# A hybrid attention block: the RMS norm's weight row multiplied into x instead of into every weight

## The chip, the cores and the metric

The kernel runs on one core of one Trainium2 chip. The metric is the device time of one launch in microseconds (us). The engines are called by the profile's names: PE (TensorE; PEld is its weight load), DVE (VectorE), ACT (ScalarE), POOL (GpSimd) and SP (SyncE, which issues the DMAs here).

## The reference

One layer of an encoder block on x of 2048 tokens by 1024 columns, all float32:

```python
def rms_norm(x, gain):
    y = x * lax.rsqrt(jnp.mean(x * x, axis=-1, keepdims=True) + EPS)
    return y * gain

h = rms_norm(x, norm_gain)            # norm_gain: 1024 numbers, one per column
proj = h @ w_in                       # 1024 x 8448: q, k, v of two mixers, gates, merge logits
# A: 8 query heads, 2 key/value heads of 64, window +-128, a sink logit
# B: 3 groups of 8 heads, (window, dilation) = (128,1), (512,4), (2048,16), joined by softmax denominators
# q and k: RMS norm per head; relative position bias; y = attention * silu(gate path)
merged = sigmoid(mg0 + b0) * (ya @ w_branch_a) + sigmoid(mg1 + b1) * (yb @ w_branch_b)
out = x + merged @ w_out
```

Since `h @ w = (x / rms) @ (gain[:, None] * w)`, the norm's weight row can be multiplied into the rows of w or into the columns of x.

## The kernel before

**Precision.** Matrix products of float32 operands are made of three float16 products: each operand is split into a high part (scaled by a power of two and rounded) and a low part (what is left). XH and XL hold the two parts of the normalized, transposed x for the whole run (columns of x on the partitions, 8 chunks, tokens along the free dimension); `wh`/`wl` and `gh`/`gl` hold those of a piece of weights.

**Start: x is prepared.** x comes in 16 tiles of 128 tokens by 1024 columns (`x_load`, 512 KB each, 14 buffers). For each tile:

- `x_square` (L427, ACT) sums the squares of each token; `x_stats` (L431, L240, DVE) and `x_newton` make the reciprocal root for a group of tiles: tiles 0 and 1, tiles 2 and 3, then groups of four. For the groups of two the Newton steps run on DVE (L254 to L256), for the groups of four on POOL (L249 to L252).
- `x_scale` (L441, DVE) multiplies the tile in place by the tokens' factors.
- `x_turn` (L447, PE) transposes it in two halves into PSUM (3 buffers `s`); `x_hi` (L450, ACT) writes XH and `x_lo` (L454, DVE) XL.

Between the transposes PE already works: the first two chunks of gate weights (`g_load`, `graw`) are prepared, and their products with the finished quarters of x (`g_step`, L288) are interleaved with the transposes of the next tiles.

**Weights.** Weights come in units of 384 columns (`w_units`, 14 of them, one attention head group each, then `w_mrg` for the merge gates) and in gate chunks of 128 columns (`w_gate`). Each is loaded raw in float32 (`w_load`, `g_load`), multiplied in place by the norm's weights `gn` (`w_gain`, L159, four pieces of two chunks of rows; `g_gain`, L303, two pieces of four; both on POOL), squared and summed on ACT (`w_square`, L198; `g_square`, L311), summed over the partitions by a matmul with ones (`norm_sum`, L173, on PE), turned into a power-of-two scale on DVE (`norm_pow`), and split (`w_hi`, L215, ACT; `w_lo`, L221, DVE; `g_hi`, `g_lo`, L333). The scale's inverse goes into later factors (`wsc`, `ih`, `im`, `imh`), and the unit's scale into the epsilon of the head norm (`sig`).

**Units.** While PE projects unit u (L617), the steps of unit u+1's weights run on the other engines. For each pair of token blocks the projections leave PSUM (L635, L647, L653), the q and k norms run (squares L660, sums L665, Newton steps on POOL, product L677 on DVE, head gain L684 on POOL, split L690 and L694, copies L699), and the transposed pieces feed the scores (L767), maxima (L782), exponentials (L790), splits (L795, L799) and values (L816). The branch outputs are gated by `YPart` (L882).

**End.** After the units, the products with the branch and merge weights (L288 into `fps`) and the output projection (L1254) follow.

**Order.** From the start to the end of the units every engine's instructions stand in an order that the code writes: each step is put into one heap with a planned time (`at(time, step)`), and steps are emitted in order of these times. Each engine then works through its own list in order. `chain` keeps the steps of one piece of weights in sequence. The x steps are planned by X_SQ, X_ST and X_CH: the first statistics at 7.8, the first scale at 9.3, each next scale 2.65 later. The loads are planned at .01 times the tile number; the load of `gn` (4 KB, 32 bytes to each partition) stands between the second and the third x tile, the first gate chunk behind the fourth. The part after the units is ordered by the framework's scheduler from its own estimates.

Of the kernel before, what the change touches and what calls it, by code (L numbers as in the profile page):

```python
# [21 lines left out]
F32 = mybir.dt.float32  # L22
# [3 lines left out]
OP = mybir.AluOpType  # L26
# [13 lines left out]
VSC = 2.0 ** -20  # L40
SX = 2.0 ** 10
SE = S + 256
# [36 lines left out]
X_G = (7.5, 15.282, 45.87)  # L79
X_GP = (2.1, 5.694, 7.094, 7.694, 8.894, 10.194)  # L80
X_W = (14.0, 38.0, 48.0, 1.1, 4.8, 5.2, 6.3, 0.6, 50.255)
X_TH = (0.8, 2.173, 3.5)
# [9 lines left out]
def block_kernel(tc, x, w_units, w_gate, w_mrg, w_out, w_bra, gain, qkg, sink, bias_a, bias_b, b_merge, out):  # L92
# [32 lines left out]
    XL = xp.tile([128, NCH, SE], F16, name="XL")  # L125
    gn = cst.tile([128, NCH], F32, name="gn")

# [20 lines left out]
    def w_load(u, parts=(0, 1, 2, 3)):  # L148
# [4 lines left out]
        for i in parts:  # L153
            nc.sync.dma_start(out=raw[:, 2 * i:2 * i + 2, :], in_=src[:, 2 * i:2 * i + 2, :])

    def gains(raw, c0, n):

        v = raw[:, c0:c0 + 2, :n]
        G.tensor_tensor(v, v, gn[:, c0:c0 + 2].unsqueeze(2).to_broadcast([128, 2, n]), OP.mult)  # L159

    def w_gain(u, i):
        gains(wtiles[u][0], 2 * i, 384 if u < NU else 256)

# [61 lines left out]
    def w_scale(u):  # L225
        for i in range(4):
            w_gain(u, i)
            w_square(u, i)
        for f in (w_sum, w_pow):
            f(u)  # L230
# [69 lines left out]

    def g_gain(c, i):
        v = gw[c][0][:, 4 * i:4 * i + 4, :]
        G.tensor_tensor(v, v, gn[:, 4 * i:4 * i + 4].unsqueeze(2).to_broadcast([128, 4, 128]), OP.mult)  # L303

    def g_square(c):
# [14 lines left out]
    def g_pow(c):  # L320
        raw, gh, gl, ps = gw[c]
        s, inv = norm_pow(ps)
        ih = ucol()
        V.tensor_scalar(ih[:], inv[:], 0.5 / SX, None, OP.mult)
        gw[c] = (gh, gl, ih, raw, s)
# [113 lines left out]
    def x_scale(t):  # L439
        i = t - groups[t][0]  # L440
        V.tensor_scalar(xts[t][:], xts[t][:], xss[groups[t]][:, i:i + 1], None, OP.mult)  # L441

# [34 lines left out]
    for t in range(XT_BUFS):  # L477
        at(.01 * t, x_load, t)
    at(.015, lambda: nc.sync.dma_start(out=gn[:], in_=gain))
    at(.035, g_load, 0)  # L480
# [27 lines left out]
    for c in range(3):  # L508
        b = X_G[c]
        if c == 2:  # L510
            at(X_G[0] + X_GP[5] + .1, g_load, c)
        chain([(b + X_GP[0] * i, g_gain, c, i) for i in range(2)]
              + [(b + d, f, c) for d, f in zip(X_GP[1:], (g_square, g_sum, g_pow, g_hi, g_lo))])
    at(X_W[0], w_load, 0)
    steps = [(X_W[2] + X_W[4], w_sum, 0), (X_W[2] + X_W[5], w_pow, 0)]
    for i in range(4):
        steps += [(X_W[1] + 1.9 * i, w_gain, 0, i), (X_W[2] + X_W[3] * i, w_square, 0, i),
                  (X_W[2] + X_W[6] + X_W[3] * i, w_hi, 0, i), (X_W[2] + X_W[6] + X_W[7] + X_W[3] * i, w_lo, 0, i)]
# [32 lines left out]
    class Unit:  # L551
# [20 lines left out]
        def scales(self):  # L572
            s, inv = wtiles[self.u][1:3]
            sig = sm.tile([128, 1], F32, name="sig")
            V.tensor_scalar(sig[:], s[:], SX, None, OP.mult)
# [4 lines left out]
            V.tensor_scalar(self.wsc[:], inv[:], 2.0 ** 6 / SX, None, OP.mult)  # L580
            ws[UNITS[self.u]] = self.wsc
# [478 lines left out]
    while t < NPAIR or heap or any(k >= t for k in fill):  # L1060
# [38 lines left out]
        if t == NPAIR - 2:  # L1099
            V.tensor_scalar(imh[:], wtiles[NU][2][:], 0.5 / SX, None, OP.mult)  # L1100
        t += 1
# [80 lines left out]
    for dc in (1, 2, 3, 4, 5, 6, 7, 0):  # L1182
# [3 lines left out]
        if own:  # L1186
            im = ucol()
            V.tensor_scalar(im[:], wtiles[u][2][:], 0.5 / SX, None, OP.mult)
        for q in range(4):
# [103 lines left out]
def _layout(x, norm_gain, w_in, q_norm_a, k_norm_a, q_norm_b, k_norm_b, sink_a, rel_bias,  # L1293
# [18 lines left out]
    bm = b_merge[0].reshape(2, 8, 128).transpose(2, 0, 1).reshape(128, 16)  # L1312
    return [x[0], w_units, w_gate, w_mrg, wo, w_bra, norm_gain.reshape(NCH, 128).T, qkg, sink_a, bias_a, bias_b, bm]

# [19 lines left out]
```

## Time and profile before

| | |
|---|---|
| time, three runs | 2017.61, 2019.15, 2013.93 us |
| median | 2017.61 us |
| span of the profiled execution (no other time is listed for it) | 2015.2 us |
| busy: PE, DVE, ACT, POOL | 1965.1, 1265.5, 1004.8, 839.3 us |
| instructions | 47585 |
| mean granted TensorE clock | 0.993 |

In rows of instructions, the first number is the start in us after the span's start, the second the duration in us; then engine, line, operation, tiles (out<-in), shapes and count; in brackets the engine's idle time before the instruction and what ended it. In lists of waits, the numbers are the total in us, how often, and the longest. In rows of stretches, the length comes first, then the busy time of PE, PEld, DVE, ACT and POOL with the count of instructions, then the granted clock, the DMA engines' share and GB/s.

### The profile page before, as it was taken

The page shows a single profiled execution, that of the slowest core. Times are in us where ns is not written, and L with a number is a line of the kernel's source. Part 1 is how long each engine was busy: PE and PEld are TensorE (multiplying, and loading weights), DVE is VectorE, ACT ScalarE, POOL GpSimd, SP SyncE. Part 2 cuts the span into 40 slices and gives each one's busy share as a digit, 9 for nine tenths or more (in the row PEclk, how much of TensorE's full clock was granted, in tenths as well). Part 3 has the DMA queues.
Part 4 walks back from the last instruction along what each step waited for, and adds up shares of the span by engine and source line. Part 5 has one row for each costly group of instructions (what it writes and reads, how often), then busy time and mean ns, then how long its engine had stood idle before and what let it go on. Part 6 is the DMA issues. An engine that isn't in the chain of part 4 may idle for free.

```text
span 2015.2 us, 47585 instructions
## 1 busy us (share of the span) xinstructions
PE 1965.1 (98%) x17666; PEld 1399.8 (69%) x17666; DVE 1265.5 (63%) x3456; ACT 1004.8 (50%) x2357; POOL 839.3 (42%) x2351
## 2 busy tenths in 40 slices
PE   6999999999999999999999999999999999999999
PEld 4567886678878898788989889896434444444444
DVE  6678877887768876677767877668572322254211
ACT  6467656765655566555666556565362221121100
POOL 4254556455647665566666666666200000000000
PEclk8999999999999999999999999999999999999999
DMA  6249976896659687486966857567551110046832
GB/s 243 79 92 175 171 151 142 152 191 142 167 117 174 134 162 155 97 178 119 183 118 133 183 119 160 99 140 169 149 182 42 48 49 31 27 141 205 268 122 89
DMA packets 560249, 276.97 MB, mean 137 GB/s; under 512 B 457744, under 2 KB 512144, under 8 KB 558480
## 3 DMA queue, kind: packets, MB, share of 16 engines
q1 hardware_dynamic: 560016, 273.93, 59.8%
q8 instruction: 138, 2.26, 0.5%
q14 instruction: 95, 0.78, 0.1%
HBM read 115.23 MB, written 48.50 MB: 81 GB/s over the span
## 4 chain that ended last, share of the span: by engine, by line
PE 79%; POOL 5%; DMA 5%; DVE 5%; issue 4%; ACT 2%; SPq 0%; POOLq 0%; DVEq 0%; ACTq 0%
PE pj L617 32%; PE fps L288 15%; PE pj L288 14%; PE fps L1254 8%; PE s L767 4%; PE pv L816 4%; DVE rw L677 1%; POOL rs_t L249 1%; POOL rs_t L250 1%; POOL rw L684 1%; DVE qss L665 1%; DMA fg<-ytd 1%; POOL rs_t L251 1%; PE s L447 1%; DMA graw<-in_w_gate_dram 1%
## 5 line engine op out<-in xcount | busy, mean ns | idle before, releaser
L617 PE MATMUL pj<-wl,XH 128*128 128x128 f16 (+2 forms) x2816 | 714.6, 268 | 0.0
L617 PE MATMUL pj<-wh,XH 128*128 128x128 f16 (+2 forms) x2816 | 708.4, 268 | 4.0 <-DVE vt L653 4.0
L617 PE MATMUL pj<-wh,XL 128*128 128x128 f16 (+2 forms) x2816 | 712.2, 269 | 0.0
L617 PEld LDWEIGHTS <-XH 128*128 128x128 f16 x5632 | 577.8, 113 | 66.8 <-issue 4.7
L617 PEld LDWEIGHTS <-XL 128*128 128x128 f16 x2816 | 316.8, 113 | 26.0
L782 DVE CUSTOM_DVE_ANT_0 pr<-s,b,ubuf 128x256 f32<-128x256 f32 (+3 forms) x512 | 218.7, 464 | 63.9 <-PE s L767 62.0
L288 PEld LDWEIGHTS <-wh 128*128 128x128 f16 x1280 | 125.7, 99 | 153.7 <-issue 7.7
L249 POOL TENSOR_TENSOR rs_t<-rs_y 128x8 f32<-128x8 f32 (+2 forms) x345 | 108.4, 314 | 209.1 <-DVE rs_y L240 151.8
L799 DVE SCALAR_TENSOR_TENSOR p<-pr,p 128x512 f16<-128x512 f32 (+2 forms) x256 | 184.2, 719 | 6.4 <-ACT p L795 5.3
L159 POOL TENSOR_TENSOR wraw<-wraw,gn 128x768 f32<-128x768 f32 (+1 forms) x80 | 108.3, 1360 | 170.5 <-DMA wraw<-in_w_mrg_dram 170.3
L684 POOL TENSOR_TENSOR rw<-rw,g 128x128 f32<-128x128 f32 (+1 forms) x224 | 137.8, 635 | 82.0 <-DVE rw L677 67.7
L1204 DVE SCALAR_TENSOR_TENSOR fg<-fg,fps 128x512 f32<-128x512 f32 x64 | 43.4, 685 | 202.7 <-PE fps L288 187.2
L677 DVE TENSOR_TENSOR rw<-rw,qr 128x512 f32<-128x512 f32 (+1 forms) x112 | 114.7, 1024 | 87.7 <-POOL vt L646 56.0
L795 ACT ACTIVATE p<-pr 128x512 f16<-128x512 f32 (+2 forms) x256 | 159.1, 622 | 11.0 <-DMA pt<-p 4.7
L635 ACT ACTIVATE rw<-pj 128x256 f32<-128x256 f32 (+1 forms) x224 | 86.6, 386 | 140.5 <-PE pj L617 136.5
L767 PE MATMUL s<-kq 128*128 128x128 f16 (+1 forms) x1856 | 147.3, 218 | 2.8 <-DMA kq<-spl 2.8
L767 PEld LDWEIGHTS <-kq 128*128 128x128 f16 x2016 | 130.1, 98 | 25.1 <-issue 3.0
L288 PE MATMUL pj<-XH,gh 128*128 128x512 f16 x384 | 146.9, 382 | 0.0
L288 PE MATMUL pj<-XL,gh 128*128 128x512 f16 x384 | 146.8, 382 | 0.0
L288 PE MATMUL pj<-XH,gl 128*128 128x512 f16 x384 | 146.6, 382 | 0.0
L699 POOL COPY spl<-spl 128x256 f16<-128x256 f16 (+1 forms) x224 | 92.6, 443 | 126.2 <-DVE spl L694 121.6
L816 PEld LDWEIGHTS <-pt 128*128 128x128 f16 x3024 | 122.0, 97 | 24.3 <-DMA pt<-p 2.4
(182 smaller groups left out, 3644.9 us busy)
## 6 DMA issues: line engine op xcount, KB each, us to landing
wraw<-in_w_units_dram SPq DMA_DIRECT2D x56, 384.0 KB, 4.8
wraw<-in_w_mrg_dram SPq DMA_DIRECT2D x24, 384.0 KB, 4.3
zd<-z SPq DMA_DIRECT2D x128, 66.0 KB, 1.9
zz<-zd SPq DMA_DIRECT2D x64, 132.0 KB, 3.1
xt<-in_x_dram SPq DMA_DIRECT2D x16, 512.0 KB, 9.7
gtd<-yo SPq DMA_DIRECT2D x32, 256.0 KB, 3.1
yo<-gtd SPq DMA_DIRECT2D x32, 256.0 KB, 3.8
ytd<-yo SPq DMA_DIRECT2D x32, 256.0 KB, 4.1
```

What stands on the lines that cost most here:

```text
L159: G.tensor_tensor(v, v, gn[:, c0:c0 + 2].unsqueeze(2).to_broadcast([128, 2, n]), OP.mult)
L249: G.tensor_tensor(tv, yv, yv, OP.mult)
L288: out.append(lambda w=w, xx=xx, ch=ch, i=i: T.matmul(ps[:], lhsT=w[:, ch, c0:c0 + 128], rhs=xx[:, ch, ts], start=(i == 0), stop=(i == n - 1)))
L617: out.append(lambda lhs=lhs, rhs=rhs, ch=ch, a=a, b=b, k=k: T.matmul(ps[:, a:b], lhsT=lhs[:, ch, :], rhs=rhs[:, ch, a:b], start=(k == 0), ...
L677: V.tensor_tensor(q, q, self.rr[:, :n].unsqueeze(2).to_broadcast([128, n, HD]), OP.mult)
L684: G.tensor_tensor(q[:, i, :un.nq, :], q[:, i, :un.nq, :], g, OP.mult)
L767: T.matmul(self.sv[j][:, o:o + k1 - k0], lhsT=q[:, h, :], rhs=kt[:, un.nq + kh + v * un.nk, k0:k1], start=(v == 0), stop=(v == 1))
L782: V.tensor_tensor_reduce(out=self.pv[:, j, self.p0:self.p0 + W], in0=self.sv[j], in1=un.bias[:, self.h0 + j, self.b0:self.b0 + W], scale=I ...
L795: A.activation(self.sp[:, :128 * n], self.pr, AF.Copy, scale=PSC)
L799: V.scalar_tensor_tensor(self.sp[:, 128 * n:], self.pr, PSC, self.sp[:, :128 * n], OP.mult, OP.subtract)
L816: T.matmul(self.po[:, j, :w], lhsT=p[:, n * j + s, :], rhs=un.v[key][:, vh, c0:c0 + w], start=(k == 0 and s == 0), stop=(k == 2 and s == n ...
L1254: T.matmul(ps[:], lhsT=m[:, ch, k, 128 * t:128 * t + 128], rhs=woh[h][w][:, ch, :], start=(i == 0), stop=(i == 23))
```

## The change

All multiplications of weights by `gn` are taken out (`gains`, `w_gain`, `g_gain` and their places in the order). Instead the norm's weight row is loaded once, the same 1024 numbers to each of the 128 partitions (`gain_load`, 512 KB written, planned between the third and the fourth x tile). `gain_scale`, planned at 6.5, finds its largest magnitude, makes a power of two from it (`pow2`, five small instructions), scales the row, and keeps that power and its inverse in `gp2` and `gi2`. `x_scale` multiplies x by the token's factor and by this row in one instruction. Where a later factor held the old scale, the power of two comes in as a second scalar of the same instruction. SX is halved.

```diff
-SX = 2.0 ** 10
+SX = 2.0 ** 9
+X_GS = 6.5
...
-    def gains(raw, c0, n):
-        v = raw[:, c0:c0 + 2, :n]
-        G.tensor_tensor(v, v, gn[:, c0:c0 + 2].unsqueeze(2).to_broadcast([128, 2, n]), OP.mult)
-    def w_gain(u, i):
-        gains(wtiles[u][0], 2 * i, 384 if u < NU else 256)
...
     def w_scale(u):
         for i in range(4):
-            w_gain(u, i)
             w_square(u, i)
...
-    def g_gain(c, i):
-        v = gw[c][0][:, 4 * i:4 * i + 4, :]
-        G.tensor_tensor(v, v, gn[:, 4 * i:4 * i + 4].unsqueeze(2).to_broadcast([128, 4, 128]), OP.mult)
...
-        V.tensor_scalar(ih[:], inv[:], 0.5 / SX, None, OP.mult)
+        V.tensor_scalar(ih[:], inv[:], 0.5 / SX, gp2[0][:], OP.mult, OP.mult)
...
     def x_scale(t):
         i = t - groups[t][0]
-        V.tensor_scalar(xts[t][:], xts[t][:], xss[groups[t]][:, i:i + 1], None, OP.mult)
+        V.scalar_tensor_tensor(xts[t][:], xts[t][:], xss[groups[t]][:, i:i + 1], gb[:], OP.mult, OP.mult)
+
+    gb = sp0.tile([128, D], F32, name="gb")
+
+    def gain_load():
+        nc.sync.dma_start(out=gb[:], in_=gain.broadcast_to([128, D]))
+
+    def gain_scale():
+        m = sm.tile([128, 1], F32, name="gm")
+        V.tensor_reduce(m[:], gb[:], AX.X, OP.max, apply_absolute_value=True)
+        s, i = pow2(m[:], "x")
+        V.tensor_scalar(gb[:], gb[:], s[:], 2.0 ** -14, OP.mult, OP.mult)
+        gp2.append(ucol())
+        gi2.append(ucol())
+        V.tensor_scalar(gp2[0][:], i[:], 2.0 ** 14, None, OP.mult)
+        V.tensor_scalar(gi2[0][:], s[:], 2.0 ** -14, None, OP.mult)
...
-    at(.015, lambda: nc.sync.dma_start(out=gn[:], in_=gain))
+    at(.025, gain_load)
+    at(X_GS, gain_scale)
...
-            steps += [(t + W_STEP[2] - W_STEP[6] + W_STEP[3] * i, w_gain, u + 1, i),
-                      (t + W_STEP[2] + W_STEP[3] * i, w_square, u + 1, i),
+            steps += [(t + W_STEP[2] + W_STEP[3] * i, w_square, u + 1, i),
...
-              + [(t + G_PREP[1] + .1 * i, g_gain, c, i) for i in range(2)]
               + [(t + d, f, c) for d, f in zip(G_PREP[2:], (g_square, g_sum, g_pow, g_hi, g_lo))])
```

The start's own gains of unit 0 and of the first three gate chunks go in the same way; `sig`, `wsc`, `imh` and `im` get `gi2` or `gp2` as `ih` does.

More of the change, by code (lines that the diff above doesn't have):

```diff
@@ L125, in block_kernel @@
     XL = xp.tile([128, NCH, SE], F16, name="XL")
-    gn = cst.tile([128, NCH], F32, name="gn")
+    gp2, gi2 = [], []
     def pow2(mx, name):
@@ L511, in block_kernel @@
             at(X_G[0] + X_GP[5] + .1, g_load, c)
-        chain([(b + X_GP[0] * i, g_gain, c, i) for i in range(2)]
-              + [(b + d, f, c) for d, f in zip(X_GP[1:], (g_square, g_sum, g_pow, g_hi, g_lo))])
+        chain([(b + d, f, c) for d, f in zip(X_GP[1:], (g_square, g_sum, g_pow, g_hi, g_lo))])
     at(X_W[0], w_load, 0)
@@ L516, in block_kernel @@
     for i in range(4):
-        steps += [(X_W[1] + 1.9 * i, w_gain, 0, i), (X_W[2] + X_W[3] * i, w_square, 0, i),
+        steps += [(X_W[2] + X_W[3] * i, w_square, 0, i),
                   (X_W[2] + X_W[6] + X_W[3] * i, w_hi, 0, i), (X_W[2] + X_W[6] + X_W[7] + X_W[3] * i, w_lo, 0, i)]
@@ L574, in scales @@
             sig = sm.tile([128, 1], F32, name="sig")
-            V.tensor_scalar(sig[:], s[:], SX, None, OP.mult)
+            V.tensor_scalar(sig[:], s[:], SX, gi2[0][:], OP.mult, OP.mult)
             self.eps = ucol()
@@ L579, in scales @@
             self.wsc = ucol()
-            V.tensor_scalar(self.wsc[:], inv[:], 2.0 ** 6 / SX, None, OP.mult)
+            V.tensor_scalar(self.wsc[:], inv[:], 2.0 ** 6 / SX, gp2[0][:], OP.mult, OP.mult)
             ws[UNITS[self.u]] = self.wsc
@@ L1099, in block_kernel @@
         if t == NPAIR - 2:
-            V.tensor_scalar(imh[:], wtiles[NU][2][:], 0.5 / SX, None, OP.mult)
+            V.tensor_scalar(imh[:], wtiles[NU][2][:], 0.5 / SX, gp2[0][:], OP.mult, OP.mult)
         t += 1
@@ L1187, in block_kernel @@
             im = ucol()
-            V.tensor_scalar(im[:], wtiles[u][2][:], 0.5 / SX, None, OP.mult)
+            V.tensor_scalar(im[:], wtiles[u][2][:], 0.5 / SX, gp2[0][:], OP.mult, OP.mult)
         for q in range(4):
@@ L1312, in _layout @@
     bm = b_merge[0].reshape(2, 8, 128).transpose(2, 0, 1).reshape(128, 16)
-    return [x[0], w_units, w_gate, w_mrg, wo, w_bra, norm_gain.reshape(NCH, 128).T, qkg, sink_a, bias_a, bias_b, bm]
+    return [x[0], w_units, w_gate, w_mrg, wo, w_bra, norm_gain, qkg, sink_a, bias_a, bias_b, bm]
 _INS = ["x", "w_units", "w_gate", "w_mrg", "w_out", "w_bra", "gain", "qkg", "sink", "bias_a", "bias_b", "b_merge"]
```

## The prediction

> **What bounds the kernel now.** I read the profile page first, then the busy time of four stretches, then what TensorE (PE) waited for, and last the first 30 us instruction by instruction.
>
> ```profile
> span 2015.2 us, 47585 instructions
> PE 1965.1 (98%) x17666; PEld 1399.8 (69%) x17666; DVE 1265.5 (63%) x3456; ACT 1004.8 (50%) x2357; POOL 839.3 (42%) x2351
> ```
>
> PE is busy 98% of the span, so a faster POOL or a slower DVE counts only where PE stands still. The next rows give, for each stretch, its length and then the busy time of PE, PE's weight loads, DVE, ACT and POOL; the cuts are at PE's last long wait of the start (27.1), at the end of the gate matmuls that run while x is prepared (82.2), and near the end of the units (1460).
>
> ```profile
> 0.00:27.10 27.10, 7.59 (x35) 5.90 (x35) 15.72 (x44) 19.07 (x33) 11.37 (x26) 0.90 0.94 359
> 27.10:82.20 55.10, 55.10 (x295) 31.94 (x296) 42.77 (x96) 35.21 (x61) 17.12 (x34) 0.95 0.18 70
> 82.20:1460.00 1377.80, 1357.99 (x14833) 1115.81 (x14831) 1028.84 (x2984) 830.36 (x2040) 793.97 (x2276) 1.00 0.72 147
> 1460.00:2015.20 555.20, 544.47 (x2508) 246.20 (x2506) 178.15 (x333) 120.14 (x224) 16.80 (x16) 0.99 0.34 110
> ```
>
> PE is idle for 19.5 us before 27.1, never in the next 55 us, for 19.8 us in the 1378 us of the units (1377.80 less 1357.99) and for 10.7 us after. The first idle time has one cause, in the list of PE's waits:
>
> ```profile
> PE s L447 <- DVE xt L441: 18.3, 4, 10.1
> ```
>
> In four waits, one of 10.1 us, PE stands before the transposes (L447) of an x tile that DVE has not yet scaled (L441). From 27.1 on PE never catches up, since it has no idle time to give back: **what the change adds to the way to the fifth scaled tile lengthens the whole kernel one for one.**
>
> **What is removed.** The multiplications by `gn` are all on POOL (min/median/max in ns, then first and last start in us):
>
> ```profile
> L159 POOL TENSOR_TENSOR wraw<-wraw,gn x80: 1037/1467/1917, 47.8 to 1636.4; 128x768 f32<-128x768 f32 x56, 128x512 f32<-128x512 f32 x24
> L303 POOL TENSOR_TENSOR wraw<-wraw,gn x18: 1030/1042/1488, 170.2 to 1376.0; 128x512 f32<-128x512 f32 x18
> L303 POOL TENSOR_TENSOR graw<-graw,gn x6: 1037/1041/1486, 10.9 to 55.4; 128x512 f32<-128x512 f32 x6
> L479 SPq DMA_DIRECT2D gn<-in_gain_dram x1: 424/424/424, 1.7 to 1.7; - x1
> ```
>
> That is 104 instructions. At about 1.4 us for those 512 to 768 wide (L159) and 1.04 us for the other 24, some 135 us of POOL go. POOL is not the bound, so this is worth only the PE waits that end on such a multiplication. PE's matmuls of the weight norms (L173) waited for these:
>
> ```profile
>   DVE yo L882: 4.9, 2
>   ACT gh L311: 2.3, 2
>   ACT wl L198: 0.8, 1
> ```
>
> L311 and L198 are the squares of the weights; each stands right behind the gain of its piece. For the first of the two at L311, the chain that ended last shows it (start us, us, what):
>
> ```profile
> 781.57 2.44 POOL wraw L303 x2
> ```
>
> Two gains run, then the square, then PE's matmul. Without the gains the square starts over 2 us sooner, more than the wait, so I take off 2.3 + 0.8 us. A third kind goes through DVE:
>
> ```profile
> 96.34 1.47 POOL L159 TENSOR_TENSOR wraw<-wraw,gn 128x768 f32<-128x768 f32 x1
> ...
> 96.38 2.11 DVE L677 TENSOR_TENSOR rw<-rw,qr 128x640 f32<-128x640 f32 x1 [1.63 <-POOL vt L646]
> ```
>
> The DVE product that starts just behind a gain stretches to 2.11 us, past the gain's end: the two engines block one another. The work behind it reaches PE late, once, at 102.45:
>
> ```profile
> 102.45 0.32 PE L617 MATMUL pj<-wh,XH 128*128 128x384 f16 x1 [0.75 <-DVE vt L653]
> ```
>
> That 0.75 us goes too. **Removed from PE's path: 2.3 + 0.8 + 0.75 = 3.9 us.** For the other 16 us of idle time in the units I take nothing: I found no gain in the last steps before them. Their bounds are 0 and, on the good side, most of them (a rival below). After 1460 us no PE wait ends on a gain; the changed list may order that part otherwise, which I leave at zero.
>
> **What is added: the way to the fifth scaled tile.** `gain_scale` stands on DVE's in-order queue ahead of the first statistics (planned time 6.5 against 7.8), and waits for the new 512 KB load of the row; behind it are queued both statistics, both Newton steps and the first scales, and PE behind those. DVE now:
>
> ```profile
> 7.00 0.17 DVE L431 TENSOR_SCALAR xss<-xss 128x2 f32<-128x2 f32 x1 [7.00 <-ACT jk L427]
> ...
> 9.17 0.75 DVE L441 TENSOR_SCALAR xt<-xt,xr 128x1024 f32<-128x1024 f32 x1
> 10.76 0.17 DVE L431 TENSOR_SCALAR xss<-xss 128x2 f32<-128x2 f32 x1 [0.84 <-ACT jk L427]
> 10.97 1.02 DVE L240 TENSOR_SCALAR rs_y<-xss 128x2 int32<-128x2 int32 x1
> 12.03 0.95 DVE L254 TENSOR_TENSOR rs_t<-rs_y 128x2 f32<-128x2 f32 x1
> ...
> 20.32 0.16 DVE L431 TENSOR_SCALAR xss<-xss 128x4 f32<-128x4 f32 x1
> 20.51 0.17 DVE L240 TENSOR_SCALAR rs_y<-xss 128x4 int32<-128x4 int32 x1
> ...
> 25.45 1.50 DVE L441 TENSOR_SCALAR xt<-xt,xr 128x1024 f32<-128x1024 f32 x1 [1.72 <-POOL xr L252]
> ```
>
> When does the row land? The new load is queued right behind the third x tile. ACT's squares show the landings of the third and the fifth:
>
> ```profile
> 8.34 1.06 ACT L427 ACTIVATE jk<-xt 128x1024 f16<-128x1024 f32 x1 [1.37 <-DMA xt<-in_x_dram]
> ...
> 12.16 1.06 ACT L427 ACTIVATE jk<-xt 128x1024 f16<-128x1024 f32 x1 [1.43 <-DMA xt<-in_x_dram]
> ```
>
> Three transfers of 512 KB landed in those 3.8 us, 1.27 us each, so the row would land at 9.6 us, or earlier as `gn`'s own load ahead of the third tile is gone; I take 9.0. Then `gain_scale`: a reduction over 1024 columns, 7 small instructions at 0.19 us (20.32 to 20.51) and a two-scalar pass of 0.75 us like L441's. The trace has no 1024-wide reduction; the row for a 1024-wide DVE pass with two tensors is
>
> ```profile
> L333 DVE SCALAR_TENSOR_TENSOR gl<-graw,ubuf,gh x3: 1278/1279/1285, 21.3 to 76.9; 128x1024 f16<-128x1024 f32 x3
> ```
>
> so 1.28 + 1.33 + 0.75 = 3.4 us. The statistics and Newton steps keep their 2.17 us (7.00 to 9.17). The first scale starts at 9.0 + 3.4 + 2.2 = 14.6 instead of 9.17: **+5.4 us**. Part of that comes back. The waits inside the next Newton steps go (L240 and L254 took 1.02 and 0.95 us instead of the usual 0.17, behind POOL's first two `graw` gains, from 10.9): -1.6. DVE's idle 0.84 us at 10.76 fills: -0.8. And each scale is now a scalar_tensor_tensor over two tensors, for which L333 is the nearest row: 1.28 instead of 0.75 us, three times before the third group's statistics (20.32): +1.6. There the shift is 5.4 - 1.6 - 0.8 + 1.6 = +4.6. The Newton steps of that group are POOL's, and wait while DVE scales:
>
> ```profile
> 20.76 0.63 POOL L249 TENSOR_TENSOR rs_t<-rs_y 128x4 f32<-128x4 f32 x1 [1.48 <-DVE rs_y L240]
> 21.47 1.12 POOL L250 TENSOR_TENSOR rs_t<-rs_t,xss 128x4 f32<-128x4 f32 x1
> ```
>
> Behind longer scales I add 0.8 us; the fifth scale itself, 1.50 us now because POOL held it, becomes 1.28 to 2.0: +0.1. **Start: +5.5 us**, with PE's transposes at 32.6 instead of 27.1. Its lower bound is +4 (the row lands at 8.3, POOL blocks nothing); a gain is excluded, since PE's wait ends on this queue. For the upper bound, the nearest row of a broadcast load is
>
> ```profile
> qg<-in_qkg_dram SPq DMA_DIRECT2D x1, 128.0 KB, 9.8
> ```
>
> 9.8 us from issue to landing; issued at 2 us this gives 11.8, 2.8 us later than I took, so +8.3.
>
> The other eleven scales cost 11 x 0.53 = 5.8 us of DVE while PE is saturated. I take zero, covered by DVE's idle time:
>
> ```profile
> 30.00:40.00 10.00, 10.00 (x55) 5.98 (x54) 8.15 (x19) 7.71 (x13) 3.85 (x12) 0.89 0.25 97
> 40.00:50.00 10.00, 10.00 (x59) 5.96 (x57) 7.11 (x14) 6.34 (x11) 4.93 (x14) 1.00 0.09 36
> ```
>
> The scales run from 25.45 to 63.8 (the last one's start), 3.49 us apart, so 2.87 in 10 us: DVE goes from 8.15 to 9.67 and from 7.11 to 8.6. The cover holds, but by 0.3 us in 10 where it is thinnest. The two-scalar forms of the small scale products replace others one for one and cost nothing; the changed constant SX costs nothing.
>
> ```profile
> L441 DVE TENSOR_SCALAR xt<-xt,xr x16: 742/746/1503, 9.2 to 63.8; 128x1024 f32<-128x1024 f32 x16
> ```
>
> The Trainium skill speaks against this edit: "VectorE: DVE Perf Modes", section "The perf-mode tier table", gives a float32 tensor_scalar in SBUF two elements a cycle and a tensor_tensor one, 1227 against 2293 ns at 2048 columns. By that ratio a scale would take an estimated 1.39 us, and the forecast would be 0.4 us later.
>
> **Sum.** 2015.2 + 5.5 - 3.9 = 2016.8 for the profiled span, that is +1.6. The span lies 2.4 us below the median of the three runs, 2017.61, and inside their spread (2013.93 to 2019.15); no other time of that execution is given. Against the median: **2019.2 us**.
>
> **Rivals.** *Slower: DVE becomes the bound of the start.* For it: the thinnest cover is 1.85 us in 10, or 0.64 us for each tile, and the scale takes 0.53 of it; L441's longest is 1.50 us, so POOL adds up to 0.75 us when it holds a scale. It decides from 0.64 us more per scale. With 0.53 + 0.75 each, DVE would need 8.15 + 3.67 = 11.8 us and 10.8 us for 10: on average 1.3 over, for 38 us: +5 us. 2019.2 + 5 = 2024.2. Against it: the gains, which held scales, go, and most scales already run at their minimum. (The skill's 1.39 us would be 0.65 more per scale, just at that point.)
>
> *Faster: POOL's relief reaches the other PE waits.* DVE and POOL hold one another all through the units (the 2.11 us row), and 135 us of POOL vanish. If 9 of the remaining 16 us go: 2019.2 - 9 = 2010.2. Against it: those waits end on other chains, such as yo at L882 with 4.9 us, and the Newton steps and products that make up POOL's other 700 us stay.
>
> **Chances.** A measurement of this kernel tells about 0.3%, 6 us, from no change. Forecast, within 6 us: 0.55. DVE-bound start, or the late broadcast on top of it: slower, 0.28. Relief: faster, 0.17. The range runs from the relief's 2010 to 2027, the DVE-bound start with the upper bound of the load (2024.2 + 2.8); that leaves about 0.1 out on each side.
>
> **What would show it.** Right: the first L441 starts near 14.6 and lasts 1.28 us; PE's first transposes start 5 to 6 us later; PE's wait on L441 grows from 18.3 to about 24; L159 and L303 are gone, as are PE's waits for L311 and L198; PE is still idle for nearly nothing from then to the units. Wrong: waits of PE for L441 after 35 us (the slower rival), PE idle far below 16 us in the units (the faster one), or a first L441 before 13 us, which would say that the row's load or its scaling was mis-sized.

## The result, and the profile after

The changed kernel takes 2011.66 us (median of 15 runs, 2008.52 to 2015.47), the kernel before beside it 2019.15 us (15 runs, 2012.73 to 2023.34). The ratio is 0.9962, with a 95% interval of 0.9952 to 0.9972: **7.5 us faster** by the medians, where 1.6 us more were forecast. A second comparison on another occasion gave 0.9975 (0.9966 to 0.9985), or 5.0 us. Below, a difference in us is the ratio less 1, times the median of before that belongs to it.

The head of the page after, and its stretches, cut where PE's last long wait of the start ends (32.22 instead of 27.10); columns as before:

```profile
span 2006.9 us, 47445 instructions
PE 1960.9 (98%) x17666; PEld 1399.4 (70%) x17666; DVE 1232.4 (61%) x3465; ACT 1003.8 (50%) x2357; POOL 704.5 (35%) x2247
```

```profile
0.00:32.22 32.22, 8.39 (x34) 6.56 (x35) 19.36 (x53) 19.64 (x34) 10.36 (x23) 1.00 0.93 368
32.22:82.20 49.98, 49.98 (x269) 29.68 (x270) 42.33 (x92) 33.15 (x57) 8.59 (x27) 1.00 0.09 35
82.20:1460.00 1377.80, 1367.95 (x14905) 1121.71 (x14903) 999.16 (x3008) 836.16 (x2050) 685.53 (x2198) 1.00 0.72 149
```

PE still has no idle time between the start and 82.2 us. In the units its idle time is 9.85 us (1377.80 less 1367.95) instead of 19.8, and DVE is busy for 30 us less (999.16 against 1028.84), though nothing was taken off DVE there. The list of PE's waits after:

```profile
PE s L450 <- DVE xss L419: 16.1, 1, 16.1
PE s L450 <- DVE xt L429: 7.1, 4, 3.3
...
PE pt L166 <- DVE yo L885: 3.3, 2, 2.3
PE pt L881 <- DVE ya L982: 3.1, 1, 3.1
PE s L770 <- DMA kq<-spl: 2.9, 1, 2.9
...
PE pv L819 <- DMA pt<-p: 0.4, 2, 0.2
...
PE pj L620 <- DVE vt L656: 0.2, 1, 0.2
```

The waits before an x tile's transposes at the start, the first two rows, sum to 23.2 us (18.3 before). Waits for squares of weights (`gh`, `wl`) are gone. So is nearly all of what PE waited for `vt`: 0.2 us instead of 4.0 + 0.6, of which the forecast had counted 0.75.

The start on DVE, and PE's transposes of the fifth tile:

```profile
9.71 1.22 DVE L438 TENSOR_REDUCE gm<-gb 128x1 f32<-128x1024 f32 x1 [9.71 <-DMA gb<-in_gain_dram]
11.72 0.75 DVE L440 TENSOR_SCALAR gb<-gb,ubuf 128x1024 f32<-128x1024 f32 x1
12.51 0.16 DVE L419 TENSOR_SCALAR xss<-xss 128x2 f32<-128x2 f32 x1
14.68 1.28 DVE L429 SCALAR_TENSOR_TENSOR xt<-xt,xr,gb 128x1024 f32<-128x1024 f32 x1
...
24.42 0.16 DVE L419 TENSOR_SCALAR xss<-xss 128x4 f32<-128x4 f32 x1
...
30.06 2.02 DVE L429 SCALAR_TENSOR_TENSOR xt<-xt,xr,gb 128x1024 f32<-128x1024 f32 x1 [1.70 <-POOL xr L244]
```

```profile
32.22 1.08 PE L450 MATMUL s<-idf,xt 128*128 128x128 f32 x4 [3.29 <-DVE xt L429]
```

This part came out nearly as worked out: 14.68 for the first scale (14.6 forecast), 1.28 us for each, 32.22 us for PE (32.6 forecast; 27.10 before). What failed is the other part, the units.

PE's matmuls stand in the same order in both kernels, so one and the same matmul can be found in both profiles. The first of the units (L617 before, L620 after) starts at 82.04 us before and at 87.69 us after; the last one ahead of PE's last wait of the units starts at 1447.34 and 1439.46 us. The changed kernel is 5.7 us late at the first, 7.9 us early at the second, and its span is 8.3 us shorter: in these two profiles the gain arises in the units. (The granted clock of 1.00 in the first two rows of stretches is not borne out by the matmuls: those of 512 columns take 0.63 us each until about 38 us and 0.38 us from then on. In the kernel before they take 0.63 us until about 32 us.)

### The profile page after: what moved, and what is told of

Same layout as the page of the kernel before. It is cut to its first block, busy times and chain, and to the rows that moved or that the text cites. A ratio compares the mean times of both kernels' runs of the same rounds, so it can differ in the third digit from the quotient of the medians.

```text
span 2006.9 us, 47445 instructions
## 1 busy us (share of the span) xinstructions
PE 1960.9 (98%) x17666; PEld 1399.4 (70%) x17666; DVE 1232.4 (61%) x3465; ACT 1003.8 (50%) x2357; POOL 704.5 (35%) x2247
## 4 chain that ended last, share of the span: by engine, by line
PE 91%; DMA 4%; DVE 2%; ACT 1%; issue 1%; POOL 1%; SPq 0%; POOLq 0%; DVEq 0%; ACTq 0%
PE pj L620 42%; PE fps L280 15%; PE pj L280 14%; PE fps L1255 8%; PE s L770 5%; PE pv L819 4%; DMA fg<-ytd 1%; PE s L450 1%; PE pt L881 1%; DMA wraw<-in_w_out_dram 1%; DMA pt<-p 1%; DMA yo<-gtd 0%; DMA wraw<-mtd 0%; DMA gb<-in_gain_dram 0%; DMA kq<-spl 0%
## 5 line engine op out<-in xcount | busy, mean ns | idle before, releaser
L620 PE MATMUL pj<-wl,XH 128*128 128x128 f16 (+2 forms) x2816 | 713.7, 268 | 0.0
L620 PE MATMUL pj<-wh,XL 128*128 128x128 f16 (+2 forms) x2816 | 711.4, 269 | 0.0
L620 PE MATMUL pj<-wh,XH 128*128 128x128 f16 (+2 forms) x2816 | 707.5, 268 | 0.2 <-DVE vt L656 0.2
L620 PEld LDWEIGHTS <-XH 128*128 128x128 f16 x5632 | 577.4, 113 | 62.0 <-issue 0.3
L620 PEld LDWEIGHTS <-XL 128*128 128x128 f16 x2816 | 316.3, 112 | 25.8
L1255 PE MATMUL fps<-woh,M 128*128 128x512 f16 x464 | 138.2, 379 | 0.0
L819 PE MATMUL pv<-vt,pt 128*128 128x65 f16 (+1 forms) x2784 | 131.7, 193 | 0.4 <-DMA pt<-p 0.4
```

The source lines that it names most:

```text
L620: out.append(lambda lhs=lhs, rhs=rhs, ch=ch, a=a, b=b, k=k: T.matmul(ps[:, a:b], lhsT=lhs[:, ch, :], rhs=rhs[:, ch, a:b], start=(k == 0), ...
L819: T.matmul(self.po[:, j, :w], lhsT=p[:, n * j + s, :], rhs=un.v[key][:, vh, c0:c0 + w], start=(k == 0 and s == 0), stop=(k == 2 and s == n ...
L1255: T.matmul(ps[:], lhsT=m[:, ch, k, 128 * t:128 * t + 128], rhs=woh[h][w][:, ch, :], start=(i == 0), stop=(i == 23))
```

## The experiments

All runs in one table: busy time of POOL and DVE in the profile, PE's idle time from 82.2 to 1460 us there, the median of the runs, and the ratio to the kernel before on the same chip.

| kernel | POOL | DVE | PE idle | median us | ratio (95%) |
|---|---|---|---|---|---|
| before (first profile) | 839.3 | 1265.5 | 19.8 | 2016.5 to 2019.2 | 1 |
| after, first | 704.5 | 1232.4 | 9.8 | 2011.66 | 0.9962 (0.9952, 0.9972) |
| after_again | 704.5 | 1232.1 | 12.4 | 2012.45 | 0.9975 (0.9966, 0.9985) |
| start_only | 845.9 | 1276.3 | 16.2 | 2022.0 | 1.0021 (1.0007, 1.0035) |
| no_gain | 703.2 | 1218.5 | 11.6 | 2004.71 | 0.9937 (0.9920, 0.9954) |
| no_w_gain | 727.0 | 1227.2 | 13.9 | 2013.06 | 0.9978 (0.9963, 0.9994) |
| no_g_gain | 809.8 | 1260.5 | 16.6 | 2011.14 | 0.9968 (0.9955, 0.9980) |
| row_first | 706.7 | 1231.9 | 12.7 | 2009.19 | 0.9958 (0.9942, 0.9973) |
| row_first_again | 704.3 | 1232.3 | 10.3 | 2009.25 | 0.9966 (0.9954, 0.9977) |
| row_filler | 704.4 | 1232.6 | 7.9 | 2008.86 | 0.9958 (0.9941, 0.9975) |
| dummy_set | 820.8 | 1233.5 | 11.3 | 2010.49 | 0.9959 (0.9943, 0.9976) |
| dummy_mul | 837.7 | 1247.6 | 11.8 | 2010.42 | 0.9967 (0.9952, 0.9982) |
| dummy_pool | 873.9 | 1259.3 | 18.0 | 2017.79 | 1.0001 (0.9989, 1.0012) |
| dummy_one | 914.1 | 1242.2 | 23.5 | 2022.4 | 1.0030 (1.0017, 1.0042) |
| dep_small | 724.4 | 1232.0 | 12.0 | 2007.52 | 0.9955 (0.9943, 0.9967) |
| dep_mul | 855.6 | 1248.9 | 12.5 | 2009.51 | 0.9963 (0.9951, 0.9975) |
| aside | 873.7 | 1257.8 | 13.4 | 2012.85 | 0.9983 (0.9975, 0.9991) |
| many_short | 874.3 | 1246.0 | 17.2 | 2020.49 | 1.0015 (0.9998, 1.0032) |
| few_long | 878.1 | 1280.1 | 21.5 | 2021.07 | 1.0021 (1.0003, 1.0038) |
| halves | 869.1 | 1260.7 | 16.5 | 2012.28 | 0.9976 (0.9959, 0.9992) |

### The two halves of the change, apart

**start_only**: the kernel before with the changed start and with POOL's multiplications kept (by a norm row of its own).

```diff
+    at(.025, gain_load)
+    at(X_GS, gain_scale)
...
-        V.tensor_scalar(xts[t][:], ..., None, OP.mult)
+        V.scalar_tensor_tensor(xts[t][:], ..., gb[:], OP.mult, OP.mult)
```

> The kernel before, with the changed kernel's start alone: the row is loaded and scaled on DVE and x_scale takes two tensors, while POOL keeps all its multiplications of the weights (so the norm's weight is in the result twice). Theory 1 (the multiplications on POOL cost the units some 13 us of waits on PE and of lowered clock, the new start costs 5): 5 us slower than before, some 2024 against 2019, PE idle about 20 us between the start and the end of the units as before. Rival (the waits of the units went because the whole sequence is shifted by the longer start, or were a matter of that one execution): no slower than before, or faster, with PE idle near 10 us in the units.

Measured: +4.2 us (1.4 to 7.1). That agrees with the forecast's +5.5 for the start.

**no_gain**: the kernel before without the multiplications.

```diff
-        gains(wtiles[u][0], 2 * i, 384 if u < NU else 256)
+        pass
...
-        G.tensor_tensor(v, v, gn[:, 4 * i:4 * i + 4].unsqueeze(2).to_broadcast([128, 4, 128]), OP.mult)
+        pass
```

> The kernel before with the multiplications by the norm's weight left out altogether (neither x nor the weights get them); x_scale and the start's loads stay as before. Theory 1: the start stays short and the units lose their waits: 13 us faster than before, some 2006. The prediction's step (only the 3.9 us of waits that end on such a multiplication go): 2015. Rival of the shift: 2015 to 2019, the other waits of the units stay.

Measured: -12.7 us (-16.1 to -9.3), where the forecast's step was -3.9. In its profile PE's transposes of the fifth tile start at 27.11 us, as before, so the gain lies behind the start. The two add up to -8.5, about what the whole change brought (-7.7 and -5.0 in the two comparisons). So the start was right, and the relief of the units was sized at a third of what it is.

**no_w_gain** and **no_g_gain** leave out only the 80 multiplications of the unit and merge weights, or only the 24 of the gate chunks (one `pass` of the two above each).

> The kernel before without the 80 POOL multiplications of the norm's weight into the unit weights; those into the gate weights stay. The unit weights are thus not multiplied by the norm's weight. Without any of the 104 it took 2004.7 us, 12.7 us less than before in the mean. Theory C: the gain follows POOL's time, 112 of 137 us are in these 80, so about 10 us go: 2008 to 2009. Theory D: it follows the few places where PE's waits end on them (the waits at 102, 885, 1088 and 1391 us, 0.75 + 0.58 + 0.84 + 0.57 us): 2.7 us go: 2016, and the waits at 785, 1140 and 1378 us stay.

> The kernel before without the 24 POOL multiplications of the norm's weight into the gate weights; those into the unit weights stay. The gate weights are thus not multiplied by the norm's weight. Theory C (the gain follows POOL's time, 25 of 137 us): about 2.3 us go: 2016 to 2017. Theory D (it follows the places): the waits for the gate weights' squares at 785 and 1378 us (1.15 + 1.11 us) go, that at 1140 us (2.15 us) as well, and the stretch at half clock of 1.7 us that followed it: 6 us go: 2012 to 2013.

Measured: -4.4 us (-7.5 to -1.2) and -6.5 us (-9.1 to -4.0). The 24 short ones, with a fifth of the time on POOL, bring no less than the 80: Theory C falls; what a multiplication costs depends on where it stands. Theory D has the sizes, but not its places: in the profile of no_w_gain the wait at 785 us is gone as well (0.11 us of it is left), though the gate multiplications are still there. The one at 1140 us is gone too, but outside the first profile of before no profile has more than 0.19 us of it, with multiplications or without (table further down).

### Is it POOL's time, or that POOL holds DVE?

**dummy_pool**, **dummy_set**, **dummy_mul** and **dummy_one** put useless POOL work into the changed kernel at the places of the removed multiplications: per piece of a unit's weights three multiplications of a scratch tile 192 wide, five memsets of it, three multiplications 128 wide, three multiplications 192 wide by a constant.

```diff
+    def w_gain(u, i):
+        for k in range(3):
+            G.tensor_tensor(v, v, ones[:, 0:2].unsqueeze(2).to_broadcast([128, 2, 96]), OP.mult)
...
+        steps += [(X_W[1] + 1.9 * i, w_gain, 0, i), (X_W[2] + X_W[3] * i, w_square, 0, i),
```

> The changed kernel, with POOL kept as busy as before: at the place of each removed multiplication POOL multiplies a small scratch tile that nobody reads, three times 128x192 for a piece of a unit and two times for a piece of a gate chunk (1.5 and 1 us by estimate). The weights' squares no longer wait for it by data. Theory 1a (the waits of the units come from POOL's time: its own queue, and DVE held while POOL reads): most of the 13 us comes back, some 2020 against the changed kernel's 2012. Rival 1b (they came from the squares waiting for the multiplied weights): within 2 us of the changed kernel, 2010 to 2014.

> The changed kernel plus POOL memsets of a small scratch tile that nobody reads, at the places of the removed multiplications (five of 128x192 for a piece of a unit's weights, four for a piece of a gate chunk), so that POOL's queue is about as long as it was, but POOL reads nothing from SBUF for it. The same with POOL multiplications took 2017.8 us. Theory A: what cost time was POOL's queue; the work behind it (qr, vt, gh) comes late. Then 2016 to 2019, PE idle for about 18 us in the units, and the waits that the multiplications brought back are there again. Theory B: what cost time was that DVE and POOL hold one another while POOL reads two operands. Then 2011 to 2013 and about 10 us of PE idle time in the units. If memsets run much shorter than the multiplications, POOL's busy time in the profile will say so, and Theory A must then be scaled by it.

> The changed kernel plus POOL multiplications of a scratch tile that nobody reads, at the places of the removed ones, as once before (2017.8 us), but two thirds as wide, so that POOL gets about as much to do as with the memsets (128 us, 2010.5 us). Theory A (the length of POOL's queue decides): with the same POOL time as with memsets the time is that of the memsets, 2010 to 2012, and the 2017.8 us came from 177 us of work. Theory B (DVE and POOL hold one another): DVE's busy time rises by 15 to 25 us over the changed kernel's 1232, and the kernel takes 2014 to 2018 us.

> The changed kernel plus POOL multiplications of the scratch tile (128x192) by a constant, at the same places: POOL reads one operand from SBUF and not two. Theory B1 (any POOL pass that reads SBUF holds DVE): DVE's busy time rises as with two operands, in proportion to POOL's added time, and the kernel takes 2014 to 2018 us. Theory B2 (only two operands do): DVE stays at 1232 to 1236 us and the kernel near the changed one, 2010 to 2012. What POOL's added time is, the profile has to say; the rows of before have no pass with one operand of that width.

The groups of added instructions on POOL (line, operation, shapes, count, busy us, mean ns, idle time before them), of dummy_pool, dummy_set, dummy_mul and dummy_one:

```profile
L190 POOL TENSOR_TENSOR scr<-scr,ones 128x192 f32<-128x192 f32 x240 | 146.0, 608 | 13.8
```

```profile
L189 POOL MEMSET scr<- 128x192 f32 x400 | 103.1, 258 | 19.3
```

```profile
L190 POOL TENSOR_TENSOR scr<-scr,ones 128x128 f32<-128x128 f32 x240 | 118.5, 494 | 13.8
```

```profile
L189 POOL TENSOR_SCALAR scr<-scr 128x192 f32<-128x192 f32 x240 | 181.7, 757 | 14.4
```

With the smaller groups for the gate chunks this is 177, 128, 143 and 221 us. The first run had seemed to settle it (dummy_pool gives the whole gain back), and the memsets, which read nothing and leave DVE at 1233.5 us, seemed to say that the holding of DVE was the cause. dummy_mul took that back: it holds DVE by 15 us (1247.6 against 1232.4) and is as fast as the changed kernel. POOL time of about the removed size, in short instructions, costs nothing. dummy_one fits neither of its theories: it holds DVE by only 10 us (1242.2) and yet has the highest ratio of all, 1.0030. So 221 us of added POOL work cost time though DVE is held less than in dummy_mul.

### Is it the squares, which wait for POOL?

In the units of before, ACT stood in front of the squares of the weights, waiting for POOL:

```profile
ACT wl L198 <- POOL wraw L159: 14.6, 11, 3.3
ACT wl L198 <- POOL vt L646: 7.7, 4, 3.0
ACT gh L311 <- POOL vt L646: 3.9, 5, 0.9
```

These 26.2 us are gone after the change, and none of the useless work brings them back. **dep_mul** is dummy_mul with that dependence, **dep_small** has the dependence almost alone, **aside** is the kernel before without it.

```diff
+        r = wtiles[u][0][:, 2 * i:2 * i + 2, 0:4]
+        G.tensor_tensor(r, r, ones[:, 0:2].unsqueeze(2).to_broadcast([128, 2, 4]), OP.mult)
```

```diff
-        G.tensor_tensor(v, v, gn[:, c0:c0 + 2]..., OP.mult)
+        for k in range(c0, c0 + 2):
+            G.tensor_tensor(scr[:, 0:n], raw[:, k, :n], gn[:, k:k + 1].to_broadcast([128, n]), OP.mult)
```

> The changed kernel with the narrower useless POOL multiplications (143 us, 2010.4 us), and behind each group of them one multiplication by 1 of four columns of the weight piece itself, so that ACT's square of the piece has to wait for POOL's queue as it did before. Theory E (ACT's in-order queue stands before the squares, and what is queued behind them, copies that PE needs, comes late): ACT's waits for POOL before the squares come back, 20 us or more in the units, and the kernel takes 2017 to 2022, as with the real multiplications and the changed start (2022.0). Theory A (POOL's time alone, with a threshold): 2011 to 2014.

> The changed kernel with only the multiplication by 1 of four columns of each weight piece on POOL, 0.2 to 0.3 us each, at the places of the removed ones: the squares wait for POOL's queue, but POOL has hardly more to do. Theory E: ACT waits for what POOL has queued ahead, a part of the 26 us (the rows before gave 11.6 us of it to work of POOL other than the multiplications); 2013 to 2017. Theory A: 2011 to 2012, as the changed kernel.

> The kernel before with the products of the weights and the norm's weight written to a scratch tile (in halves, as float16), so that POOL reads and multiplies as before, but ACT's squares use the raw weights and don't wait. The weights are thus not multiplied by the norm's weight. Theory E: near the kernel without any multiplication (2004.7 us): 2004 to 2009, though POOL is as busy as before. Theory A (the passes themselves cost it): 2013 to 2018.

ACT's waits in dep_mul:

```profile
ACT wl L201 <- POOL wraw L192: 21.8, 17, 3.5
ACT wl L201 <- POOL vt L668: 7.6, 5, 2.3
ACT gh L317 <- POOL vt L668: 5.1, 6, 1.3
```

They are back, with 34.5 us, and the kernel is still as fast as the changed one (0.9963). In aside they are gone, and only 3.4 us of the 12.7 come; halves, below, has instructions of the same widths and does have these waits, and gains no less (4.8 us). Theory E falls from both sides: ACT's wait there is idle time that costs nothing.

### Is it the length of one instruction?

**many_short** has four multiplications of 128 for a piece of a unit, **few_long** two of 384; **halves** is the kernel before, whole, with each multiplication in two instructions.

```diff
-        v = raw[:, c0:c0 + 2, :n]
-        G.tensor_tensor(v, v, gn[:, c0:c0 + 2]..., OP.mult)
+        for k in range(c0, c0 + 2):
+            v = raw[:, k, :n]
+            G.tensor_tensor(v, v, gn[:, k:k + 1].to_broadcast([128, n]), OP.mult)
```

> The changed kernel with useless POOL multiplications of 128x128, four for each piece of a unit's weights (three cost nothing) and two for a piece of a gate chunk: some 180 us, 0.49 us each. Theory T (the total decides): 2016 to 2021, as with 177 us in instructions of 0.61 us (2017.8). Theory L (the length of one instruction decides): 2009 to 2013.

> The same with 384 elements in one instruction (about 0.97 us by the row of the products in halves), two for a piece of a unit's weights and one for a piece of a gate chunk: some 180 us again. Theory T: as with the many short ones, 2016 to 2021. Theory L: clearly slower than those, 2018 to 2024.

> The kernel before with each multiplication of the weights in two instructions of half the width, in place: the same computation, some 175 instead of 137 us of POOL, each instruction 0.65 to 0.97 instead of 1.0 to 1.5 us. Theory T: slower than before by 0 to 4 us. Theory L: faster than before by 2 to 6 us.

many_short (180 us of added work) and few_long (179 us) are equally slow, as Theory T has it; halves is 4.8 us faster than before (1.6 to 8.3) with 30 us more on POOL, as Theory L has it. The first two do not differ in length alone: few_long reads two broadcast operands and writes float16. And the traces show a second reason why they cannot decide it. POOL in many_short, and what follows:

```profile
1440.08 9.04 POOL L190 TENSOR_TENSOR scr<-scr,ones 128x128 f32<-128x128 f32 x17
1449.08 1.75 POOL L990 TENSOR_TENSOR zz<-zz,bm_e 128x256 f32<-128x256 f32 x3
...
1450.30 0.82 DVE L996 TENSOR_TENSOR ya<-zz 128x256 f32<-128x256 f32 x1 [4.77 <-POOL zz L990]
...
1451.71 0.69 PE L896 MATMUL pt<-idf,ya 128*128 128x128 f32 x2 [7.47 <-DVE ya L997]
```

Seventeen useless multiplications stand in a row on POOL ahead of `zz`, and PE waits 7.47 us for what comes of it, where it waits 3.1 in the kernels before and after. They belong to the merge weights: the real ones wait for the load of those and come later, the useless ones wait for nothing. few_long has the same (8.59 us), and dummy_pool 6.43 us; dummy_set, dummy_mul and dep_mul, which cost nothing, have 3.1 us. A good part of what these three slow ones cost is thus of their own making (3.4 to 5.5 us of wait beyond the 3.1, where they are 5 to 12 us slower than the changed kernel), and Theory T is not shown by them. In dummy_one a row of them stands there too, but PE waits only 3.7 us; what that kernel costs lies elsewhere. halves stands: at more POOL time, and with ACT waiting before the squares as before (35.9 us), shorter real instructions are worth 4.8 us.

### The start, and PE's clock

**row_first** and **row_first_again** load the row ahead of the first x tile.

```diff
-    at(.025, gain_load)
+    at(-.01, gain_load)
```

> The changed kernel with the row's load queued ahead of the first x tile instead of behind the third. The row lands near 4.5 us and is scaled while DVE has nothing else; x lands 1.3 us later. The first x_scale then starts near 10.6 instead of 14.7 us. If what the start adds lengthens the kernel one for one: 4 us faster than the changed kernel, some 2007.5. If not (something else sets when PE becomes busy for good): within 1 us of it.

> The changed kernel with the row's load ahead of the first x tile, once more, beside the changed kernel on the same chip. The start loses 1.0 instead of 5.6 us. If the units then give back as much as in the changed kernel, it takes 4.6 us less than that; if a later start alone already spares part of the waits in the units (PE idle there was 12.7 against 9.9 us in the two profiles), 1 to 3 us less.

PE's transposes of the fifth tile:

```profile
28.91 1.08 PE L450 MATMUL s<-idf,xt 128*128 128x128 f32 x4 [3.31 <-DVE xt L429]
```

That is 3.3 us sooner than after the change. The medians are 2.5 and 3.2 us below the changed kernel's, with ratios whose intervals overlap with its own: less than the 4 us expected, the best guess at a kernel better than both, but not told apart from the changed one.

**after_again** is the changed kernel, for the spread between executions.

> The changed kernel as it is, for the comparison with the row's load first on the same chip: a ratio to before of 0.996, as measured before (0.9952 to 0.9972). Its profile shows how far the waits in the units vary from one execution to the next: Theory V says that the waits at about 171, 292, 395 and 622 us and the stretches at half clock differ from those of the first profile though the kernel is the same; else they are the same within 0.1 us.

PE's waits in its units, by the same groups as above:

```profile
PE pt L166 <- DVE yo L885: 3.3, 2, 2.2
PE pt L881 <- DVE ya L982: 3.1, 1, 3.1
PE s L770 <- DMA kq<-spl: 2.9, 1, 2.9
PE pv L819 <- DMA pt<-p: 2.6, 2, 1.6
```

Theory V holds: `pv` has 2.6 us where the first execution had 0.4, so waits of this size at about 171 and 395 us come and go with the execution. And the clock differs. The stretch around the wait of 2.3 us for `yo` at 514 us (granted clock third from the end), after_again first, then the first profile of the same kernel:

```profile
510.00:520.00 10.00, 7.81 (x57) 6.17 (x56) 7.91 (x29) 6.58 (x19) 5.26 (x23) 0.90 0.98 224
520.00:530.00 10.00, 10.00 (x95) 8.42 (x93) 7.83 (x34) 6.69 (x18) 3.20 (x14) 0.93 0.39 95
```

```profile
510.00:520.00 10.00, 7.73 (x66) 6.62 (x65) 7.82 (x32) 7.38 (x18) 5.14 (x23) 1.00 0.95 211
520.00:530.00 10.00, 10.00 (x111) 9.12 (x111) 8.92 (x42) 6.11 (x18) 4.04 (x18) 1.00 0.72 170
```

The same wait was followed by half the clock in the one and not in the other. 10 us at 0.90 and 10 at 0.93 are 1.7 us lost. The trace has it as one piece of 3.41 us at half clock; after this wait, which is 2.1 to 3.4 us long in all 20 profiles, 14 of them have it.

**row_filler** is row_first with 16 useless matmuls ahead of PE's last wait of the units.

```diff
+            if self.chunk == 7 and self.q == 3:
+                for k in range(16):
+                    T.matmul(self.ps[:], lhsT=XH[:, k % 8, 0:128], rhs=XH[:, k % 8, 0:512], start=True, stop=True)
```

> The changed kernel with the row's load first, plus 16 useless matmuls of 512 columns (about 3.5 us at full clock) ahead of the transposes of the last query chunk, which PE has to wait 3.08 us for at about 1441 us. Their result is overwritten. Theory K: a wait of some 3 us costs more than its length, since in most profiles the granted clock then drops to half for 3.41 us (1.7 us lost). Then the wait is gone, the clock stays at 1.00 from 1440 to 1460 us, and the kernel takes 0 to 1.5 us less than without the filler, 2009.2 us. Rival: the clock drops there for another reason than PE's wait. Then the drop is there with the filler too, and the kernel takes 0.4 us more (3.5 less 3.08).

The stretch around that wait, in row_first, then in row_filler:

```profile
1440.00:1450.00 10.00, 8.71 (x34) 3.79 (x35) 6.55 (x12) 4.78 (x7) 0.42 (x1) 0.83 0.56 174
```

```profile
1440.00:1450.00 10.00, 10.00 (x51) 5.01 (x50) 5.94 (x11) 3.33 (x5) 0.91 (x2) 1.00 0.57 183
```

Without the wait the clock stays at 1.00 there, as Theory K has it. That this saves time is not shown: 2008.86 against 2009.19 us is too close to tell. PE's next long wait, some 25 us later, is longer with the filler, and the half clock around it lasts 6.83 us instead of 3.41 (row_first, then row_filler):

```profile
1466.26 0.58 PE L280 MATMUL fps<-YH,wh 128*128 128x512 f16 x1 [2.63 <-ACT YH L1124]
```

```profile
1471.17 0.59 PE L280 MATMUL fps<-YH,wh 128*128 128x512 f16 x1 [8.07 <-ACT YH L1127]
```

## Why the prediction was right or wrong

**The start was right.** First scale 14.68 for 14.6; the row landed at 9.71 (9.0 taken) and its scaling took 2.8 us (9.71 to 12.51) for 3.4, two misses that cancel; Newton steps 2.17 us (12.51 to 14.68), as taken; third group's statistics 24.42 for 24.9; the fifth scale 2.02 us, the upper end given; PE at +5.1 for +5.5. By itself the changed start cost 4.2 us. How late PE is varies with the execution: in the eleven profiles with this start and the row at its place, the fifth tile's transposes begin 3.5 to 6.7 us later than before, around the forecast, but also below its lower bound of 4.

**DVE's cover held.** PE is busy for all of the 49.98 us up to 82.2 and never waits for an x tile after 33 us. The slower rival fell.

**The step that failed is "For the other 16 us of idle time in the units I take nothing".** The three kinds of waits that it named went, 3.9 us as forecast. But 10 us of idle time went, in the second execution 7.4 (19.8 less 12.4). In before's trace the rest are waits such as

```profile
885.13 0.22 PE L617 MATMUL pj<-wh,XH 128*128 128x128 f16 x1 [0.58 <-DVE vt L653]
...
1140.94 0.22 PE L617 MATMUL pj<-wh,XH 128*128 128x128 f16 x1 [2.15 <-DVE vt L653]
```

which both executions after lack; no multiplication stood in the last steps before them. Looking for a gain there was too narrow a test: by no_gain, the multiplications cost 12.7 us. PE's waits (us) in front of the same matmuls in more profiles show which ones come with the multiplications. before, start_only and halves have all of them, no_w_gain only the 24 of the gate chunks, no_g_gain only the 80 of the units, the last three none:

| PE waits for, at (us, in before) | before | start_only | halves | no_w_gain | no_g_gain | after | after_again | no_gain |
|---|---|---|---|---|---|---|---|---|
| `vt`, 102 | 0.75 | 0.37 | 1.08 | - | 0.44 | - | - | - |
| `gh`, 785 | 1.15 | 1.17 | 0.96 | 0.11 | 0.10 | - | - | - |
| `vt`, 885 | 0.58 | 0.58 | 0.74 | 0.58 | - | - | - | - |
| `wl`, 1088 | 0.84 | 0.86 | - | - | 0.69 | - | - | - |
| `vt`, 1140 | 2.15 | - | - | - | - | - | - | - |
| `gh`, 1378 | 1.11 | 1.03 | 0.93 | 0.43 | 0.31 | - | - | - |
| `vt`, 1391 | 0.57 | 0.57 | - | 0.56 | 0.08 | - | - | - |

The forecast counted those at 102, 785, 1088 and 1378 us. It missed those at 885 and 1391 us, 1.15 us together, which stay with the gate multiplications and go without them. Two of these do stand on POOL's queue ahead of the wait at 885 us, only 13 us ahead, followed there by Newton steps:

```profile
872.21 2.22 POOL L303 TENSOR_TENSOR wraw<-wraw,gn 128x512 f32<-128x512 f32 x2
```

The longest, at 1140 us, stands in the first profile of before alone (0.19 us at most in the other 19), so it is not shown to come from the multiplications. The waits that repeat sum to 3.7 to 5.0 us in the first three; the 12.7 us are more than these waits show. The faster rival named this ("POOL's relief reaches the other PE waits", 2010.2 us), and the argument against it, that those waits end on other chains, did not weigh against 135 us of POOL.

**A term was missing: the clock behind a wait.** The forecast took a wait at its length. In before's profile two waits of the units were followed by half clock,

```profile
1140.00:1150.00 10.00, 9.06 (x81) 7.33 (x81) 9.40 (x32) 5.13 (x14) 7.26 (x22) 0.83 1.05 253
...
1450.00:1460.00 10.00, 8.99 (x35) 3.96 (x36) 6.13 (x11) 4.05 (x6) 0.14 (x1) 0.83 0.56 160
```

1.7 us lost in each of these stretches; in the first profile after, none. Idle time (10.0 us) and these two (3.4 us) make 13.4 us; less the 5.1 of the start this is the 8.3 us between the spans (2015.2 and 2006.9). That it comes out so well is in part luck: these are two single executions, the wait at 1140 us is among the terms, and the part after 1460 us is left out. Over all 20 profiles, PE is at half clock for 0 to 10.2 us between 82.2 and 1460 us in the ten of kernels as fast as the changed one or faster, and for 6.8 to 17.1 us in the six of kernels about as slow as the one before. Half of such a time is lost where PE works, which speaks for the clock as a part of the gain; no single profile gives its size.

**What stays open** is by which way the real multiplications cost 12.7 us (9.3 to 16.1). Shown not to be enough: 128 to 168 us of POOL time in instructions of 0.26 to 0.49 us, DVE held by 17 us, ACT standing 34 us before the squares. Shown to matter: the length of the real ones, by halves, for 4.8 us. It fits that DVE loses 47 us to them (1265.5 less 1218.5 without any), but whether it is that, or the Newton steps that stand behind a long one on POOL, was not told apart. The page "SBUF — State Buffer" of the Trainium skill, section "SBUF: two separate sides", has GpSimd and VectorE lock each other out of a shared port pair for a whole instruction when the VectorE one runs in a two-port perf mode, or when it has two inputs in SBUF and the GpSimd one reads SBUF. The runs agree as to reading: memsets, which read nothing, add 1 us to DVE's time (1233.5 against 1232.4), multiplications by a constant 10 us, and those of two operands 15 to 48 us.

## What to carry to other kernels

Side work on an engine that is 40% busy is not free: leave it out whole in a run before you cost its removal from the waits that name it. Useless work put in its place is a poor stand-in where the real work waits for something: look in the trace for where it runs before you believe its time. Look for the same wait in a second execution before you put it down to the change: the longest one here, 2.15 us, was in one profile of 20. And when PE waits for 2 to 3 us, count up to 1.7 us more for the clock.

## What was not expected of the hardware

- A wait of PE of 2.1 to 3.4 us, the one at 514 us, was followed by 3.41 us at half clock in 14 of 20 profiles, 1.7 us lost each time. The page "TensorE: Matmul & The Clock Gate" of the Trainium skill, Part 1, "The HAM clock gate", gives half clock after at least one idle window of about 3.4 us, with a window that runs free. The length and the chance agree with the trace; but here waits shorter than a window were enough.
- A POOL multiplication of 192 columns by a constant takes longer than one by a tensor: 757 against 608 ns.
- On POOL, one instruction of 384 elements takes 967 ns and three of 128 take 1.45 us (483 ns each), yet many_short and few_long, with the same total, hold DVE by 14 and 48 us (1246.0 and 1280.1 against 1232.4). Their operands differ too, so the length alone is not shown to be the reason.
